# Two blocks of a transformer-like network on one core: the recurrence's gates as tanh of three fp32r products, and a fixed place on VectorE for the recurrence's second part

## The chip, the cores and the metric

One Trainium2 chip, one core. The metric is the device time of one execution in microseconds (us). The kernel takes and returns 512 tokens of width 1024 in float32.

## What is computed

The reference runs two blocks one after the other. The first (spatial gating, a gated delta rule over 64-token chunks, a mixture of 32 experts) is not touched by the change. The second puts 16 learned tokens ahead of the 512, so T = 528, and computes from the normalized tokens in parallel an attention with 8 query and 2 key heads, and a gated linear recurrence in both directions of time. Their results are merged by two gates, projected, and followed by a feed-forward layer. The recurrence is the part that matters here. For each of two directions:

```python
def rg_lru(xc, wa, ba, wx, bx, lam, reverse):
    r = sigmoid(einsum('btnc,ncd->btnd', xb, wa) + ba)   # xb: xc in 8 blocks of 128 channels
    i = sigmoid(einsum('btnc,ncd->btnd', xb, wx) + bx)
    log_a = 8.0 * r * log_sigmoid(lam)
    a = exp(log_a)
    u = sqrt(-expm1(2.0 * log_a)) * (i * xf)
    h = scan of h[t] = a[t] * h[t-1] + u[t], along time or against it
```

`xc` is a convolution over four neighbouring tokens of a projection of the input. A sigmoid is (1 + tanh(x/2)) / 2.

## The kernel before

The program is written in Python that records instructions. Tiles come from pools: `bufs` is how many buffers a name has in turn, and an instruction that writes a buffer waits until the reads of its last contents are done. In the stage of interest (`block2`, lines 1563 to 1650) the order of TensorE's instructions is the order in which they are recorded. The order on VectorE, ScalarE and SP is made by a planner, which goes by the order of recording and by when it reckons that an instruction's operands are there. Two helpers tie it: `act` (line 90) keeps ScalarE's table functions in the order of recording, and `after` puts one instruction behind others on its engine.

Matrix products that have to be exact are made with `mm3` (lines 198 to 200): both operands are split into an upper part in fp32r and a remainder (`split`: a copy on ScalarE, line 90, and a subtraction on VectorE, line 170), and three products are summed in PSUM. The views `by_turns` and `unturned` interleave the two halves of the columns, so that neighbouring columns of a product come from different halves.

The stage is a loop over n = 0 to 7. Turn n is called head n here. It joins parts of generators, each of which stops at its `yield`s:

- `gates`: three projections of 128 columns for the merge gates and the recurrence's output gate, 24 passes of 512 columns each.
- `attention` of head n: the scores for two blocks of 128 queries (`weights`; L198 to L200 into `psD`), the row maxima (L2127, L2128), the exponential (`pr`), its normalization (L2133, L2135), and in `turned` the transposes (L2141 for the 16 learned tokens, L2146 for the others) with their split into `PThi` and `PTlo`; the same again for the other two blocks; one turn later the product with the values, and one more turn later the sum with the recurrence (`ao`, L2164) and its split into `ga` and `rn`, called the mix here.
- `rnn_x` of n + 1: the projection of block n + 1 (48 passes of 264 columns), its evacuation in two halves to `xr`, and the convolution `xc` on VectorE (L2027, L2029).
- `rnn_gates` of n: eight f32 products (L2047) of 264 columns into four `psD` tiles: for each direction `rg`, then `ig`, evacuated by ScalarE as sigmoids. Then `ig` is multiplied with `xc` (L2050).
- `rnn` of n - 1, in two parts. The first makes tanh, exponential and square of the decay on ScalarE and L2093 on VectorE. The second takes two roots on ScalarE, then multiplies (L2099), scans (L2102), and adds both directions (L2104, L2105).

In a middle turn TensorE does: first projection, product with the values of head n - 1, gates of n, scores, second projection, transposes, third projection, scores, projection of block n + 1, transposes.

PSUM has two buffers of `psD` (two banks each), which the gates and the scores share, and two banks each of `psA` and `psB`. `rg`, `ig`, `wg`, `xr` and `xc` have two buffers, the root's tile `th` one. The split weights have two buffers, `whi` and `wlo`; the raw ones four, which SP loads in order.

Of the kernel before, what the change touches and what calls it, by code (L numbers as in the profile page):

```python
# [9 lines left out]
FT = mybir.dt.float32  # L10
FR = mybir.dt.float32r
I32 = mybir.dt.int32
BF = mybir.dt.bfloat16
AF = mybir.ActivationFunctionType
OP = mybir.AluOpType
# [14 lines left out]
TOKS = [slice(t * 128, (t + 1) * 128) for t in range(NT)]  # L30
# [23 lines left out]
def halves(x):  # L54

    return x.rearrange("p (s c) -> p s c", s=2)


def by_turns(x):

    return x.rearrange("p (s c) -> p c s", s=2)


def unturned(x):

    return x.rearrange("p (c s) -> p s c", s=2)
# [9 lines left out]
class Net:  # L76
# [1913 lines left out]
    def rnn_start(self, p, vec):  # L1990

        nc = self.nc
        x = vec[:, 72:88]
        cl = p.tile([128, 2, 16], FT, name="cl")
        y = p.tile([128, 16], FT, name="cl_y")
        c = cl[:, 0, :]
        nc.vector.scalar_tensor_tensor(y, x, -1.0, x, op0=OP.mult, op1=OP.min)
        self.act(y, y, AF.Exp)
        self.log1p_unit(p, c, y, 16)
        nc.vector.tensor_scalar(y, x, 0.0, None, op0=OP.min)  # L2000
        nc.vector.tensor_tensor(c, y, c, OP.subtract)
        nc.vector.tensor_scalar(c, c, 8.0, None, op0=OP.mult)
        nc.vector.tensor_scalar(cl[:, 1, :], c, -1.0, None, op0=OP.mult)
        return cl

    def rnn_x(self, p, n, vec, xT):

        nc, I = self.nc, self.I
        T = META + S
        H = T // 2  # L2010
        nhi, nlo = xT
        wg = p.tile([128, 2, 2, 128], FT, name="wg")
        nc.sync.dma_start(wg[:, 0], I["rg_wa_2"][0, :, n].rearrange("d c e -> c d e"))
        nc.sync.dma_start(wg[:, 1], I["rg_wx_2"][0, :, n].rearrange("d c e -> c d e"))
        hi, lo = self.wchunk(I["w_in_2"][0], 0, NK, 1536 + n * 128, 128)
        xr = p.tile([128, T + 3], FT, name="xr")
        nc.vector.memset(xr[:, 0:2], 0.0)
        nc.vector.memset(xr[:, T + 2:], 0.0)
        for j in range(2):
            js = slice(j * H, (j + 1) * H)  # L2020
            ps = self.psA.tile([128, 512], FT, name="psA")
            for k in range(NK):
                self.mm3(ps[:, :H], hi[:, k, :], lo[:, k, :], by_turns(nhi[:, k, js]), by_turns(nlo[:, k, js]),
                         k == 0, k == NK - 1)
            self.act(halves(xr[:, 2 + j * H:2 + (j + 1) * H]), unturned(ps[:, :H]), AF.Copy)
        c = p.tile([128, T], FT, name="xc")
        nc.vector.tensor_scalar(c, xr[:, 0:T], vec[:, n:n + 1], vec[:, 32 + n:33 + n], op0=OP.mult, op1=OP.add)  # L2027
        for j in range(1, 4):
            nc.vector.scalar_tensor_tensor(c, xr[:, j:j + T], vec[:, 8 * j + n:8 * j + n + 1], c,  # L2029
                                           op0=OP.mult, op1=OP.add)  # L2030
        return c, wg

    def rnn_gates(self, p, n, vec, x, meanwhile=lambda: None):

        nc = self.nc
        T = META + S
        H = T // 2
        c, wg = x
        rg = p.tile([128, 2, T], FT, name="rg")
        ig = p.tile([128, 2, T], FT, name="ig")  # L2040
        for d in range(2):
            if d:
                meanwhile()
            for w, dst, bias in ((0, rg, 40), (1, ig, 56)):
                ps = self.psD.tile([128, 2, 512], FT, name="psD")
                for j in range(2):
                    nc.tensor.matmul(ps[:, j, :H], wg[:, w, d, :], c[:, j * H:(j + 1) * H], start=True, stop=True)  # L2047
                self.act(dst[:, d, :].rearrange("p (a b) -> p a b", a=2), ps[:, :, :H], AF.Sigmoid,
                         bias=vec[:, bias + 8 * d + n:bias + 8 * d + n + 1])
        nc.vector.tensor_tensor(ig, ig, c[:, None, :].to_broadcast([128, 2, T]), OP.mult)  # L2050
        return rg, ig

    def gates(self, p, n, xT, rn, ga):
# [25 lines left out]
    def rnn(self, p, n, cl, st, rn):  # L2079

        nc = self.nc
        T = META + S
        rg, ig = st
        u = p.tile([128, 2, T], FT, name="th", bufs=1)
        for d in range(2):
            q = 8 * d + n
            r, t = rg[:, d, :], u[:, d, :]
            self.act(t, r, AF.Tanh, scale=cl[:, 1, q:q + 1])
            self.act(r, r, AF.Exp, scale=cl[:, 0, q:q + 1])

            a2 = p.tile([128, T], FT, name="a2", bufs=1)
            self.act(a2, r, AF.Square)
            nc.vector.scalar_tensor_tensor(t, a2, 1.0, t, op0=OP.add, op1=OP.mult)  # L2093
        yield
        for d in range(2):
            self.act(u[:, d, :], u[:, d, :], AF.Sqrt, scale=0.0625)
        for d in range(2):
            t, g, r = u[:, d, :], ig[:, d, :], rg[:, d, :]
            nc.vector.tensor_tensor(g, g, t, OP.mult)  # L2099
            if d:  # L2100
                t, g, r = t[:, ::-1], g[:, ::-1], r[:, ::-1]
            nc.vector.tensor_tensor_scan(t, r, g, 0.0, op0=OP.mult, op1=OP.add)  # L2102
        f = u[:, 0, META:]
        nc.vector.tensor_tensor(f, f, u[:, 1, META:], OP.add)  # L2104
        nc.vector.tensor_tensor(rn[n], rn[n], f, OP.mult)  # L2105
        yield

    def attention(self, tp, h, kv, rn, ga, gp, mix):
        nc = self.nc
        H = (META + S) // 2  # L2110
        khi, klo, vhi, vlo, qs = (kv[n] for n in ("khi", "klo", "vhi", "vlo", "qs"))
        g = h // 4
        qf = tp.tile([128, S], FT, name="qf")
        nc.sync.dma_start(qf, self.q_d[h])
        q = [tp.tile([128, S], FR, name="q" + n) for n in ("hi", "lo")]
        self.split(*q, qf)

        Phi = tp.tile([128, NT + 1, S], FR, name="PThi", bufs=1)
        Plo = tp.tile([128, NT + 1, S], FR, name="PTlo", bufs=1)
# [18 lines left out]
        def turned(w):  # L2138
            for t, ps, pf in w:
                pm = ps[:META, 0, H:H + 128]  # L2140
                nc.tensor.transpose(pm, pf[:, 0:META], self.ident)  # L2141
                self.split(Phi[:META, 0, TOKS[t]], Plo[:META, 0, TOKS[t]], pm)
            for t, ps, pf in w:
                pt = self.psB.tile([128, 4, 128], FT, name="psB")
                for b in range(NT):
                    nc.tensor.transpose(pt[:, b, :], pf[:, META + b * 128:META + (b + 1) * 128], self.ident)  # L2146
                self.split(Phi[:, 1:, TOKS[t]], Plo[:, 1:, TOKS[t]], pt)

        for t in (0, 2):
            w = [weights(t), weights(t + 1)]  # L2150
            yield
            turned(w)
            if t == 0:
                yield
# [179 lines left out]
```

## Time and profile before

| | |
|---|---|
| median of 3 runs | 1913.13 us (1912.49 to 1913.63) |
| the profiled execution | 1913.31 us, span 1911.5 us |
| TensorE (PE) busy | 1804.0 us, 94% of the span |
| weight loads (PEld) | 1362.2 us, 71% |
| VectorE (DVE) busy | 990.3 us, 52% |
| ScalarE (ACT) busy | 708.9 us, 37% |
| GpSimd (POOL) busy | 31.3 us, 2% |
| TensorE's clock, mean | 0.988 of full speed |
| the stage with the recurrence | about 1236 to 1545 us of the span |

Times within the span are counted from its first instruction. A matmul is recorded from its start to its modelled end, and the next one starts before that, so the distance of two starts is what a pass costs. Neighbouring VectorE and ScalarE instructions overlap in the same way. In brackets stands how long the engine was idle before an instruction, and what ended that.

### The profile page before, as it was taken

Reading aid. Unit: us, or ns where it says so; the run is one execution under the profiler, and the core shown is the slowest. Engines: PE = TensorE matmul, PEld = TensorE weight load, DVE = VectorE, ACT = ScalarE, POOL = GpSimd, SP = SyncE. Lnnn points to the kernel's source line nnn. Section 1 sums busy time; section 2 is a strip of 40 time slices with the busy share of each in tenths; the row PEclk is TensorE's granted clock in tenths of the full one; section 3 lists DMA queues with packets and bytes.
Section 4 is the critical chain, followed back from the end, with each engine's and each line's share of the span. In section 5 each row is a group of like instructions: output and inputs, shape, how many; then the busy total and the mean of one; then the engine's idle time right before and its main releaser. Section 6 shows DMA issues by size and latency. Waiting matters only on the chain. (4 is left out here: it accounts for less than half of the span.)

```text
span 1911.5 us, 23909 instructions
## 1 busy us (share of the span) xinstructions
PE 1804.0 (94%) x9309; PEld 1362.2 (71%) x9309; DVE 990.3 (52%) x1834; ACT 708.9 (37%) x1157; POOL 31.3 (2%) x39
## 2 busy tenths in 40 slices
PE   6999999989999899999898979999999999999999
PEld 5787888868898744433343337888888778888887
DVE  6843787745466623222121259658878763333332
ACT  5343444424333322111010126467677733323322
POOL 0000000100000000000000000000000000000000
PEclk9999999989999899999999999999999999999999
DMA  8645776875378689999999873432221233333331
GB/s 255 99 117 101 121 93 82 156 175 77 90 271 332 243 347 423 424 425 425 424 425 425 368 279 122 137 89 83 78 66 56 88 101 110 100 104 105 99 122 66
DMA packets 251988, 368.20 MB, mean 193 GB/s; under 512 B 31328, under 2 KB 193665, under 8 KB 227938
## 3 DMA queue, kind: packets, MB, share of 16 engines
q1 hardware_dynamic: 241218, 342.79, 56.3%
q10 hardware_dynamic: 7632, 16.78, 2.3%
q0 software_dynamic: 3024, 7.09, 1.0%
q8 instruction: 74, 1.21, 0.3%
q14 instruction: 40, 0.33, 0.0%
HBM read 348.51 MB, written 22.04 MB: 194 GB/s over the span
## 5 line engine op out<-in xcount | busy, mean ns | idle before, releaser
L90 ACT ACTIVATE whi<-raw 128x1024 fp32r<-128x1024 f32 (+1 forms) x203 | 233.4, 1155 | 417.4 <-PE psA L199 266.8
L170 DVE TENSOR_TENSOR wlo<-raw,whi 128x1024 fp32r<-128x1024 f32 (+1 forms) x195 | 249.5, 1280 | 243.2 <-ACT whi L90 229.5
L1289 PE MATMUL psB<-mwt,XT 128*64 128x512 f32 x1008 | 233.7, 598 | 7.9 <-DMA mwt<-in_w 5.5
L1289 PEld LDWEIGHTS psB<-mwt,XT 128*64 128x64 f32 x1008 | 76.6, 138 | 153.1 <-issue 135.3
L200 PE MATMUL psA<-hT_hi,wlo 128*128 128x512 f32 (+1 forms) x456 | 176.2, 386 | 10.0 <-DVE wlo L170 10.0
L199 PE MATMUL psA<-hT_lo,whi 128*128 128x512 f32 (+1 forms) x456 | 177.6, 389 | 0.0
L198 PE MATMUL psA<-hT_hi,whi 128*128 128x512 f32 (+1 forms) x456 | 176.1, 386 | 0.9 <-ACT whi L90 0.9
L1354 DVE TENSOR_TENSOR res<-res,psA 128x512 f32<-128x512 f32 x128 | 79.3, 679 | 125.0 <-PE psA L1349 125.0
L1322 PE MATMUL psB<-mwt,hbT 128*64 128x512 f32 x480 | 118.0, 596 | 21.1 <-DMA mwt<-in_w 19.8
L198 PE MATMUL psA<-hn_hi,whi 128*128 128x512 f32 (+1 forms) x368 | 136.5, 371 | 0.2 <-ACT hn_hi L90 0.2
L199 PE MATMUL psA<-hn_lo,whi 128*128 128x512 f32 (+1 forms) x368 | 136.4, 371 | 0.3 <-DVE hn_lo L2198 0.3
L200 PE MATMUL psA<-hn_hi,wlo 128*128 128x512 f32 (+1 forms) x368 | 136.3, 370 | 0.0
L198 PE MATMUL psA<-xn_hi,whi 128*128 128x512 f32 (+1 forms) x320 | 109.4, 342 | 0.4 <-ACT qx L90 0.4
L1298 DVE TENSOR_TENSOR sl<-sl,psB 128x512 f32<-128x512 f32 x16 | 11.0, 688 | 188.0 <-PE psB L1289 188.0
L200 PE MATMUL psA<-xn_hi,wlo 128*128 128x512 f32 (+1 forms) x320 | 108.2, 338 | 0.0
L199 PE MATMUL psA<-xn_lo,whi 128*128 128x512 f32 (+1 forms) x320 | 108.1, 338 | 0.0
L1322 PEld LDWEIGHTS psB<-mwt,hbT 128*64 128x64 f32 x480 | 36.1, 136 | 97.0 <-issue 58.0
L200 PEld LDWEIGHTS psA<-hT_hi,wlo 128*128 128x128 f32 (+1 forms) x456 | 86.3, 189 | 22.7 <-DVE wlo L170 11.0
L198 PEld LDWEIGHTS psA<-hT_hi,whi 128*128 128x128 f32 (+1 forms) x456 | 86.1, 189 | 13.6 <-ACT whi L90 1.3
L199 PEld LDWEIGHTS psA<-hT_lo,whi 128*128 128x128 f32 (+1 forms) x456 | 86.1, 189 | 11.9
L90 ACT ACTIVATE XT<-psA 128x512 f32<-128x512 f32 x32 | 17.5, 594 | 205.0 <-PE psA L1266 199.5
L199 PEld LDWEIGHTS psA<-hn_lo,whi 128*128 128x128 f32 x368 | 69.6, 189 | 9.5 <-DVE hn_lo L2198 0.5
(571 smaller groups left out, 3489.7 us busy)
## 6 DMA issues: line engine op xcount, KB each, us to landing
mwt<-in_w SPq DMA_DIRECT2D x188, 1024.0 KB, 20.1
raw<-in_w_in SPq DMA_DIRECT2D x108, 512.0 KB, 7.1
raw<-in_w_ffn_in SPq DMA_DIRECT2D x44, 512.0 KB, 3.9
raw<-in_w_ffn_out SPq DMA_DIRECT2D x22, 512.0 KB, 3.6
raw<-in_w_pa SPq DMA_DIRECT2D x8, 512.0 KB, 6.1
raw<-in_w_pb SPq DMA_DIRECT2D x8, 512.0 KB, 4.9
raw<-in_w_o SPq DMA_DIRECT2D x8, 512.0 KB, 11.8
raw<-in_w_out SPq DMA_DIRECT2D x8, 512.0 KB, 3.6
```

What stands on the lines that cost most here:

```text
L90: ins = self.nc.scalar.activation(out, in_, func, **kw)
L170: return self.nc.vector.tensor_tensor(lo, x, hi.bitcast(FT), OP.subtract)
L198: nc.tensor.matmul(out, whi, xhi, start=first, stop=False)
L199: nc.tensor.matmul(out, whi, xlo, start=False, stop=False)
L200: nc.tensor.matmul(out, wlo, xhi, start=False, stop=last)
L1289: nc.tensor.matmul(ps[CAP * i:CAP * (i + 1), :], XT[:, r0 + k, CAP * i:CAP * (i + 1)], w_, start=(r0 + k == 0), stop=(r0 + k == NK - 1))
L1298: nc.vector.tensor_tensor(so, so, h[1], OP.mult)
L1322: nc.tensor.matmul(pys[half][CAP * i:CAP * (i + 1), :], hT[:, r0 + k, CAP * i:CAP * (i + 1)], ws[i][:, k, half * 512:(half + 1) * 512], st ...
L1354: nc.vector.tensor_tensor(x, x, unturned(ps), OP.add)
```

## The change

`rnn_gates` makes the gates with `mm3` from split weights and a split `xc`, and evacuates them with tanh(x/2) through the view by turns. `rnn_x` therefore splits the gates' weights (into `wghi`, one buffer, and a second tile named `wg`) and `xc` (into a second tile named `xr` and `xclo`, one buffer); `xc` has one buffer instead of two. The constants take over the halves and the ones: the decay's factor is halved and also given as bias, the gate biases are halved once, the root's scale is a quarter of what it was, and `ig` is multiplied as (ig + 1) * c. Behind the two roots a tanh of one column is added. The first product of each direction in the second part is put behind the last lower part of the attention weights (`self.low`).

```diff
--- before.py
+++ after.py
@@ -1999,7 +1999,9 @@
         self.log1p_unit(p, c, y, 16)
         nc.vector.tensor_scalar(y, x, 0.0, None, op0=OP.min)
         nc.vector.tensor_tensor(c, y, c, OP.subtract)
-        nc.vector.tensor_scalar(c, c, 8.0, None, op0=OP.mult)
+        nc.vector.tensor_scalar(c, c, 4.0, None, op0=OP.mult)
+
+        nc.vector.tensor_scalar(vec[:, 40:72], vec[:, 40:72], 0.5, None, op0=OP.mult)
         nc.vector.tensor_scalar(cl[:, 1, :], c, -1.0, None, op0=OP.mult)
         return cl
 
@@ -2012,6 +2014,8 @@
         wg = p.tile([128, 2, 2, 128], FT, name="wg")
         nc.sync.dma_start(wg[:, 0], I["rg_wa_2"][0, :, n].rearrange("d c e -> c d e"))
         nc.sync.dma_start(wg[:, 1], I["rg_wx_2"][0, :, n].rearrange("d c e -> c d e"))
+        ws = p.tile([128, 2, 2, 128], FR, name="wghi", bufs=1), p.tile([128, 2, 2, 128], FR, name="wg")
+        self.split(*ws, wg)
         hi, lo = self.wchunk(I["w_in_2"][0], 0, NK, 1536 + n * 128, 128)
         xr = p.tile([128, T + 3], FT, name="xr")
         nc.vector.memset(xr[:, 0:2], 0.0)
@@ -2023,19 +2027,21 @@
                 self.mm3(ps[:, :H], hi[:, k, :], lo[:, k, :], by_turns(nhi[:, k, js]), by_turns(nlo[:, k, js]),
                          k == 0, k == NK - 1)
             self.act(halves(xr[:, 2 + j * H:2 + (j + 1) * H]), unturned(ps[:, :H]), AF.Copy)
-        c = p.tile([128, T], FT, name="xc")
+        c = p.tile([128, T], FT, name="xc", bufs=1)
         nc.vector.tensor_scalar(c, xr[:, 0:T], vec[:, n:n + 1], vec[:, 32 + n:33 + n], op0=OP.mult, op1=OP.add)
         for j in range(1, 4):
             nc.vector.scalar_tensor_tensor(c, xr[:, j:j + T], vec[:, 8 * j + n:8 * j + n + 1], c,
                                            op0=OP.mult, op1=OP.add)
-        return c, wg
+        cs = p.tile([128, T + 3], FR, name="xr")[:, 0:T], p.tile([128, T], FR, name="xclo", bufs=1)
+        self.split(*cs, c)
+        return c, cs, ws
 
     def rnn_gates(self, p, n, vec, x, meanwhile=lambda: None):
 
         nc = self.nc
         T = META + S
         H = T // 2
-        c, wg = x
+        c, (chi, clo), (whi, wlo) = x
         rg = p.tile([128, 2, T], FT, name="rg")
         ig = p.tile([128, 2, T], FT, name="ig")
         for d in range(2):
@@ -2044,10 +2050,13 @@
             for w, dst, bias in ((0, rg, 40), (1, ig, 56)):
                 ps = self.psD.tile([128, 2, 512], FT, name="psD")
                 for j in range(2):
-                    nc.tensor.matmul(ps[:, j, :H], wg[:, w, d, :], c[:, j * H:(j + 1) * H], start=True, stop=True)
-                self.act(dst[:, d, :].rearrange("p (a b) -> p a b", a=2), ps[:, :, :H], AF.Sigmoid,
+                    js = slice(j * H, (j + 1) * H)
+                    self.mm3(ps[:, j, :H], whi[:, w, d, :], wlo[:, w, d, :], by_turns(chi[:, js]), by_turns(clo[:, js]),
+                             True, True)
+                self.act(dst[:, d, :].rearrange("p (a s c) -> p a s c", a=2, s=2),
+                         ps[:, :, :H].rearrange("p a (c s) -> p a s c", s=2), AF.Tanh, scale=0.5,
                          bias=vec[:, bias + 8 * d + n:bias + 8 * d + n + 1])
-        nc.vector.tensor_tensor(ig, ig, c[:, None, :].to_broadcast([128, 2, T]), OP.mult)
+        nc.vector.scalar_tensor_tensor(ig, ig, 1.0, c[:, None, :].to_broadcast([128, 2, T]), op0=OP.add, op1=OP.mult)
         return rg, ig
 
     def gates(self, p, n, xT, rn, ga):
@@ -2085,18 +2094,21 @@
         for d in range(2):
             q = 8 * d + n
             r, t = rg[:, d, :], u[:, d, :]
-            self.act(t, r, AF.Tanh, scale=cl[:, 1, q:q + 1])
-            self.act(r, r, AF.Exp, scale=cl[:, 0, q:q + 1])
+            self.act(t, r, AF.Tanh, scale=cl[:, 1, q:q + 1], bias=cl[:, 1, q:q + 1])
+            self.act(r, r, AF.Exp, scale=cl[:, 0, q:q + 1], bias=cl[:, 0, q:q + 1])
 
             a2 = p.tile([128, T], FT, name="a2", bufs=1)
             self.act(a2, r, AF.Square)
             nc.vector.scalar_tensor_tensor(t, a2, 1.0, t, op0=OP.add, op1=OP.mult)
         yield
         for d in range(2):
-            self.act(u[:, d, :], u[:, d, :], AF.Sqrt, scale=0.0625)
+            self.act(u[:, d, :], u[:, d, :], AF.Sqrt, scale=0.25 ** 3)
+
+        self.act(self.small.tile([128, 1], FT, name="warm"), cl[:, 0, 0:1], AF.Tanh)
         for d in range(2):
             t, g, r = u[:, d, :], ig[:, d, :], rg[:, d, :]
-            nc.vector.tensor_tensor(g, g, t, OP.mult)
+
+            self.after(nc.vector.tensor_tensor(g, g, t, OP.mult), self.low)
             if d:
                 t, g, r = t[:, ::-1], g[:, ::-1], r[:, ::-1]
             nc.vector.tensor_tensor_scan(t, r, g, 0.0, op0=OP.mult, op1=OP.add)
@@ -2144,7 +2156,7 @@
                 pt = self.psB.tile([128, 4, 128], FT, name="psB")
                 for b in range(NT):
                     nc.tensor.transpose(pt[:, b, :], pf[:, META + b * 128:META + (b + 1) * 128], self.ident)
-                self.split(Phi[:, 1:, TOKS[t]], Plo[:, 1:, TOKS[t]], pt)
+                self.low = self.split(Phi[:, 1:, TOKS[t]], Plo[:, 1:, TOKS[t]], pt)
 
         for t in (0, 2):
             w = [weights(t), weights(t + 1)]
```

## Rows read from the trace of the kernel before

PE is TensorE, DVE VectorE, ACT ScalarE. Head 4 is a middle turn.

**Rows 1.** busy time: stretch, length, each engine (instructions), TensorE clock, DMA

```profile
1370.26:1404.95 34.69, 33.60 (x197) 29.14 (x195) 27.77 (x52) 25.53 (x45) 0.00 (x0) 1.00 0.27 77
```

**Rows 2.** waits of TensorE, 1236 to 1545 us: total, times, longest

```profile
PE psD L198 <- ACT rg L90: 5.4, 6, 1.0
PE psD L198 <- DVE PTlo L170: 3.0, 2, 1.8
```

**Rows 3.** timeline of TensorE, head 4: start, length, instruction, idle before

```profile
1380.16 3.89 PE L2047 MATMUL psD<-xc,wg 128*128 128x264 f32 x16
1385.02 0.38 PE L198 MATMUL psD<-kThi,qhi 128*128 128x264 f32 x1 [0.96 <-ACT rg L90]
...
1391.65 0.67 PE L2141 MATMUL psD<-ident,pr 128*16 128x128 f32 x2
```

**Rows 4.** timeline of TensorE, head 1

```profile
1276.93 3.89 PE L2047 MATMUL psD<-xc,wg 128*128 128x264 f32 x16
1280.72 0.38 PE L198 MATMUL psD<-kThi,qhi 128*128 128x264 f32 x1
```

**Rows 5.** timeline of TensorE, head 4's last projection passes

```profile
1368.01 0.28 PE L199 MATMUL psA<-xn_lo,whi 128*128 128x264 f32 x1
1368.12 0.28 PE L200 MATMUL psA<-xn_hi,wlo 128*128 128x264 f32 x1
```

**Rows 6.** timeline of ScalarE, head 4

```profile
1369.36 1.28 ACT L90 ACT_TABLE_LOAD   x1
...
1371.74 0.37 ACT L90 ACTIVATE xr<-psA 128x264 f32<-128x264 f32 x1
...
1379.13 1.28 ACT L90 ACT_TABLE_LOAD   x1 [1.56 <-DVE th L2102]
1381.25 0.70 ACT L90 ACTIVATE rg<-psD,vec 128x528 f32<-128x528 f32 x1 [0.83 <-PE psD L2047]
...
1383.74 0.63 ACT L90 ACTIVATE ga<-ao 128x512 fp32r<-128x512 f32 x1 [0.90 <-DVE xr L2018]
1384.28 0.68 ACT L90 ACTIVATE rg<-psD,vec 128x528 f32<-128x528 f32 x1
...
1388.22 1.28 ACT L90 ACT_TABLE_LOAD   x1 [2.18 <-DVE m L2128]
1389.52 0.79 ACT L90 ACTIVATE pr<-psD,m,qs 128x528 f32<-128x528 f32 x1
```

**Rows 7.** timeline of VectorE, head 4

```profile
1371.33 1.33 DVE L2099 TENSOR_TENSOR ig<-ig,th 128x528 f32<-128x528 f32 x2 [0.28 <-ACT th L90]
1372.58 0.55 DVE L2027 TENSOR_SCALAR xc<-xr,vec 128x528 f32<-128x528 f32 x1
...
1376.67 2.38 DVE L2102 TENSOR_TENSOR_SCAN th<-rg,ig 128x528 f32<-128x528 f32 x2
...
1383.04 0.67 DVE L2164 TENSOR_TENSOR ao<-ao,rn 128x512 f32<-128x512 f32 x1
...
1384.41 0.69 DVE L170 TENSOR_TENSOR rn<-ao,ga 128x512 fp32r<-128x512 f32 x1 [0.68 <-ACT ga L90]
1385.59 1.26 DVE L2050 TENSOR_TENSOR ig<-ig,xc 128x1056 f32<-128x1056 f32 x1 [0.49 <-ACT ig L90]
...
1388.00 0.28 DVE L2128 SCALAR_TENSOR_TENSOR m<-m,qs 128x1 f32<-128x1 f32 x2
...
1391.41 0.49 DVE L2135 TENSOR_SCALAR pr<-pr,s 128x528 f32<-128x528 f32 x1
```

**Rows 8.** VectorE's groups, 1236 to 1545 us: count, busy us, mean ns

```profile
L170 DVE TENSOR_TENSOR qlo<-qf,qhi 128x512 fp32r<-128x512 f32 x8 | 5.4, 677 | 1.8 <-ACT qhi L90 1.8
```

**Rows 9.** timelines of ScalarE and TensorE, the stage's tail

```profile
1520.52 1.28 ACT L90 ACT_TABLE_LOAD   x1 [2.97 <-DVE rn L2105]
...
1522.99 0.72 ACT L90 ACTIVATE rg<-rg,cl 128x528 f32<-128x528 f32 x1
...
1537.01 0.48 PE L198 MATMUL psD<-whi,ga 128*128 128x512 f32 x1 [2.01 <-ACT ga L90]
```

## The prediction

> **What bounds the kernel now.** Only the stage of the second block is touched in which the eight heads of attention and the eight blocks of the recurrence run together; I read it in this order. First the busy time of one steady head, from one pair of transposes to the same pair a head later [rows 1]: 34.69 us, of which TensorE is busy 33.60, VectorE 27.77 and ScalarE 25.53, at full granted clock. So TensorE sets the pace and VectorE is the next. Then the list of TensorE's waits [rows 2]: one line stands out, the first score matmul that waits for ScalarE's evacuation of a gate, 6 times, 5.4 us. Then that place in the timelines of TensorE, ScalarE and VectorE for head 4 [rows 3, 6, 7]. The reader should see three things.
>
> One: the gates' sixteen passes start at 1380.16 and the scores at 1385.02, 4.86 us later, the last 0.96 idle [rows 3]. In head 1, which has no earlier head's mix to split, the same passes start at 1276.93 and the scores at 1280.72, 3.79 us [rows 4]. The difference of 1.07 is ScalarE's order: the mix's upper part (`ga<-ao`) stands ahead of the second direction's `rg`, and it starts only at 1383.74, when VectorE's sum (1383.04 and 0.67 long) is there [rows 6, 7].
>
> Two: ScalarE loads three activation tables per head, 1.28 us each, at 1369.36 (root), 1379.13 (sigmoid) and 1388.22 (exponential) [rows 6]. Only the third delays something: the row maxima are scaled at 1388.28 [rows 7], and the exponential starts at 1389.52. The second weights are normalized at 1391.41 + 0.49 = 1391.90 [rows 7]; TensorE is at their transposes at 1391.65 [rows 3] and waits there about 0.3.
>
> Three: from 1371.33 to 1388.28 VectorE has almost no gap: products, convolution, lower parts, two scans, two weight splits, four elementwise steps, the gates' product, the maxima [rows 7]. The sigmoid's table load waited for the scans (they end at 1379.05), since the gate buffer is the one that they read [rows 6, 7].
>
> **The change, part by part.** The sum is made against the profiled execution, 1913.31 us with a span of 1911.5; the median of the runs is 1913.13, so they can be used alike.
>
> *Gate matmuls.* Eight f32 products, recorded as sixteen passes that occupy 3.89 us [rows 3], become 24 fp32r passes. Such passes of 264 columns start 0.11 us apart [rows 5]: 24 x 0.113 = 2.70. But there are two score buffers, so the third gate waits for the first one's evacuation: six passes 0.68; evacuation starts 0.2 later (1381.25 less 1380.16 leaves 1.09, of which four passes are about 0.9) and lasts 0.70 as now [rows 6], or 0.79, what the exponential takes that reads PSUM in the same pattern [rows 6]; 0.05 to release; third gate 0.68; 0.2; 0.70 to 0.79; 0.05. Together 3.25 to 3.45; I take 3.4. Against 3.79 that is 0.4 gained. Against 4.86 it is 1.46, if ScalarE no longer holds `rg` behind the mix. I take that it doesn't: the gate is ready about 2.6 us after the block's start, the mix's sum about 4.9 after it (1385.1, worked out with the last rival but one), so a planner that takes what is ready first has them the other way round. The reverse is a rival.
>
> Each pass has its weight load, 195 in a head and 29.14 us busy [rows 1]; passes with loads start 0.11 apart all the same [rows 5], so the eight more loads cost nothing of their own.
>
> *Sigmoid to tanh.* Tanh and exponential follow each other without a load at the tail, 1520.52 to 1522.99 [rows 9]; the load ahead of that tanh serves both. So the loads at 1379.13 and 1388.22 become one, issued by the new tanh on one element behind the roots. That one costs 1.28 where ScalarE has nothing urgent (behind the attention weights' upper parts), and the exponential starts 1.28 earlier relative to the maxima. The load occupies 1.28 and the next instruction starts at once (1388.22 + 1.28, then 1389.52) [rows 6]. The Trainium skill, ScalarE: Activation LUTs, What ACT_TABLE_LOAD costs, adds a drain of 1380 ns to each switch; by it the exponential would start 2.66 us earlier, TensorE's 1.8 per head would come through, and the time be the first rival's 1900.5. The trace disagrees: 0.02 from the load's end to the exponential, so 1.28 stands.
>
> *Splits.* Per head ScalarE gets two more copies (0.63 each, as the mix's copy of that size [rows 6]) and VectorE two more subtractions (0.68 each, start to start about 0.62), by the queries' split of the same size [rows 8]. ScalarE's 1.26 is paid by the 1.28 saved. The weights' split can go into VectorE's pauses around the exponentials, if not it costs 0.62; it is taken as 0. The convolution's split lies between the convolution and the gates, so its 0.62 lies in the dense stretch. The weights' load now waits for the previous split instead of the gates two blocks back; SP issues it in order, with other weight loads behind it, but that split is done most of a head before the next one is wanted, so 0. The biases' halving, 16-column work before the stage, 0. The product with (gate + 1) is taken at the 1.26 of the product that it replaces [rows 7]; nothing shows the other form at this width.
>
> *The tie.* The two products (1.33 [rows 7]) no longer run ahead of the convolution, but behind the last lower part. They ran in a pause in which VectorE waited for the second half of `xr` (1371.74 + 0.37 = 1372.11 [rows 6]). Convolution and lower parts therefore come about 0.4 earlier, and the scans later: their start moves from 1376.67 by -0.45 + 1.25 + 0.62 to 1378.1, their end to 1380.5. The gates' first evacuation, ready at about 1380.6, still just misses it. This tie alone gains nothing: TensorE waited for lower parts only twice, 3.0 us in all [rows 2], at the end of the stage, not in steady heads.
>
> *Sum.* VectorE's stretch from 1372.58 to 1388.28 was 15.70, with pauses of 0.68 and 0.49 [rows 7]. With the products (1.25) and the split (0.62) in and the pauses out it is 16.40, begun at 1372.11: the maxima are ready at 1388.5, 0.2 later than now. The exponential starts then, 1.0 earlier than 1389.52, and the second weights are normalized at 1390.9. TensorE, 1.46 earlier, would be there at 1390.2, so it waits for VectorE: a steady head gains 1.0 to 1.1, not 1.46 + 0.3. Five steady heads (2 to 6): 5.3. Head 1: 0.4 + 0.3 = 0.7. Head 7, whose gates lie on both sides of another product: 1.0. Head 0, where the longer way from convolution to gates eats most: 0.3. The tail: the last tanh's load, which waited for the last scan's product (1520.52), goes, and TensorE there waited 2.01 for the mix [rows 9]: 1.28, less some 0.3 for weight splits behind the new load, so 1.0. Together 8.3, so I forecast 1905.0.
>
> **The rivals.**
> *VectorE isn't the limit.* The planner puts the maxima ahead of the mix's steps, or the split of c in a pause. Then a steady head gains 1.46 + 0.3, say 1.8, five of them 9.0; with head 1's 0.7, head 7's 1.8 and 1.3 at the ends that is 12.8: 1900.5. For it: the mix is needed much later. Against: its steps come earlier in the program than the maxima. The same time would follow if a table load held ScalarE for longer than its record, which no row shows; 0.02 of the chance below is for that.
> *The load is only moved.* If the new tanh goes straight behind the roots, the second `xr` is out 1.5 later (the load and one short instruction), and VectorE's stretch with it: the maxima at 1390.0 and the exponential 0.5 later than now. Five heads lose 0.5, the ends gain 2: 1913.5. Against it: `xr` and the upper parts are earlier in the program and ready by then.
> *The mix stays ahead of the gate (slower).* With the stretch longer, the sum ends at 1383.71 + 1.4 = 1385.1 instead, the copy (0.54), `rg` and the release follow, and the scores start at 1386.4, 1.4 later than now. Less 0.3 for the transposes, each of five steady heads loses 1.1, head 7 about 0.8, less 2 at the ends: 1917.6. It decides as soon as the sum ends later than 1384.4 and the order is as now.
> *c is split late.* If its lower part is placed behind the scans (1381), the gates' second pass waits about 0.7; but that is what TensorE waits at the transposes anyway, so it changes the place of the wait and not the forecast.
>
> **How the numbers follow.** Forecast 0.42, VectorE not the limit 0.28, moved load 0.16, mix ahead 0.14. The range runs from 1897 (the second case, with 3.5 us for the forms that no row shows and the weights' split in a pause) to 1914.5 (past the moved load) and leaves out the slower case. A measurement tells about 0.2% (3.8 us) from no change. Faster by more: the first two cases, 0.70; within: the moved load and the milder part of the mix ahead, 0.18; slower: the rest, 0.12.
>
> **What would show it.** Two table loads per head, none ahead of the exponentials; gates' fp32r passes 0.113 apart; scores 3.3 to 3.5 after the gates' start, `rg` ahead of the mix's copy on ScalarE; scans ending near 1380.5 on this scale; a wait of TensorE at the transposes for the normalized weights of about 0.7. Steady heads of about 33.6 would bear out the sum; heads of 34.7 or more, with the mix's copy still ahead of `rg`, or `xr` behind a table load, would prove it wrong.

## The result, and the profile after

| | before | after |
|---|---|---|
| median (runs) | 1913.13 us (9) | 1921.78 us (9) |
| profiled execution, span | 1913.31, 1911.5 us | 1919.51, 1917.6 us |
| TensorE's clock, mean | 0.988 | 0.982 |

The ratio is 1.0055, 95% interval 1.0041 to 1.0069: the change makes the kernel slower by 8.65 us, by more than 0.2%. The forecast was 1905.0.

The loss lies in the stage with the recurrence. From head 0's gates to the first transposes of the last projection's result it took 308.55 us before (1241.21 to 1549.76) and 319.29 after (1236.53 to 1555.82): 10.74 more. The stages ahead of it were 4.68 shorter in the profile after. Of the change there lie only 16-column work and the first head's splits, and the kernel before and e7_tiles_before, whose code is the same up to there, reach head 0's gates at 1241.21 and 1245.63; so that is what one execution differs from another. The starts of the gates show where in the stage it goes (distance from gates n to gates n + 1, and from head 7's gates to those transposes; the lower rows belong to experiments):

| kernel | 0 | 1 | 2 | 3 | 4 | 5 | 6 | 7 to the end |
|---|---|---|---|---|---|---|---|---|
| before | 35.72 | 33.94 | 34.60 | 34.69 | 34.70 | 34.68 | 31.06 | 69.16 |
| after | 35.73 | 33.47 | 35.46 | 36.39 | 35.45 | 36.55 | 34.01 | 72.23 |
| e1_tiles | 35.73 | 33.48 | 34.86 | 34.31 | 34.33 | 34.32 | 31.40 | 69.01 |
| e15_scans_first | 36.88 | 33.48 | 34.90 | 34.47 | 34.44 | 34.47 | 31.60 | 69.20 |
| e9_tiles_notie | 35.73 | 34.70 | 35.39 | 37.08 | 34.69 | 37.07 | 32.29 | 72.17 |
| e13_last_head | 35.73 | 33.05 | 34.14 | 33.62 | 33.62 | 33.61 | 30.69 | 68.65 |

Only head 1 got shorter, by 0.5: it has no earlier scans to wait for, and its scores come 3.36 after its gates instead of 3.79. TensorE's waits of after (1236 to 1545 us; total, times, longest), which answer to [rows 2]:

```profile
PE psD L198 <- ACT rg L90: 12.3, 6, 2.1
PE psD L198 <- DVE PTlo L170: 3.4, 2, 1.8
PE psD L198 <- ACT whi L90: 2.6, 1, 2.6
```

The one wait that the change was to shorten is 12.3 us instead of 5.4, and it sits in another place: ahead of the third gate, no longer ahead of the scores. Of the 12.3, 1.8 lie in head 0, which waited 1.7 there before too; heads 2 to 6 wait 2.1 each. TensorE in head 4 of after, beside [rows 3]:

```profile
1377.58 0.28 PE L198 MATMUL psD<-xr,wghi 128*128 128x264 f32 x1
...
1381.19 0.38 PE L198 MATMUL psD<-xr,wghi 128*128 128x264 f32 x1 [2.10 <-ACT rg L90]
...
1382.93 0.38 PE L198 MATMUL psD<-kThi,qhi 128*128 128x264 f32 x1
...
1390.00 0.38 PE L2153 MATMUL psD<-ident,pr 128*16 128x128 f32 x2
```

Twelve passes, two gates, are through within 1.5 us. Then TensorE stands for 2.10, because the first gate is still in its PSUM buffer. The scores come 5.35 after the gates' start; before it was 4.86, and 3.4 was forecast. Why the evacuation is late is on ScalarE, beside [rows 6]:

```profile
1366.58 1.28 ACT L90 ACT_TABLE_LOAD   x1
1367.88 1.18 ACT L90 ACTIVATE th<-th 128x528 f32<-128x528 f32 x2
1369.06 1.28 ACT L90 ACT_TABLE_LOAD   x1
1370.36 0.20 ACT L90 ACTIVATE warm<-cl 128x1 f32<-128x1 f32 x1
1370.46 0.37 ACT L90 ACTIVATE xr<-psA 128x264 f32<-128x264 f32 x1
...
1380.44 0.70 ACT L90 ACTIVATE rg<-psD,vec 128x528 f32<-128x528 f32 x1 [4.37 <-DVE th L2114]
1381.04 0.69 ACT L90 ACTIVATE ig<-psD,vec 128x528 f32<-128x528 f32 x1
1382.17 0.70 ACT L90 ACTIVATE rg<-psD,vec 128x528 f32<-128x528 f32 x1 [0.44 <-PE psD L200]
1382.77 0.62 ACT L90 ACTIVATE wghi<-wg 128x512 fp32r<-128x512 f32 x1
1383.30 0.69 ACT L90 ACTIVATE ig<-psD,vec 128x528 f32<-128x528 f32 x1
...
1384.35 0.64 ACT L90 ACTIVATE ga<-ao 128x512 fp32r<-128x512 f32 x1
...
1386.55 0.79 ACT L90 ACTIVATE pr<-psD,m,qs 128x528 f32<-128x528 f32 x1 [1.56 <-DVE m L2140]
```

Three things. ScalarE is idle for 4.37 us ahead of the first `rg`, and what ends it is `th`, a scan: the new `rg` goes into the buffer that the scans of the head before read as their factor. The second table load stands straight behind the roots, so the second half of `xr` waits for it. And the two forecast gains are there: the mix's copy is behind the second `rg`, and no load stands ahead of the exponential. VectorE, beside [rows 7]:

```profile
1370.87 0.55 DVE L2031 TENSOR_SCALAR xc<-xr,vec 128x528 f32<-128x528 f32 x1 [2.25 <-ACT xr L90]
...
1374.97 0.69 DVE L2111 TENSOR_TENSOR ig<-ig,th 128x528 f32<-128x528 f32 x1
1375.59 0.69 DVE L170 TENSOR_TENSOR xclo<-xc,xr 128x528 fp32r<-128x528 f32 x1
1376.21 1.24 DVE L2114 TENSOR_TENSOR_SCAN th<-rg,ig 128x528 f32<-128x528 f32 x1
1377.38 0.67 DVE L2111 TENSOR_TENSOR ig<-ig,th 128x528 f32<-128x528 f32 x1
1377.97 1.20 DVE L170 TENSOR_TENSOR wlo<-raw,whi 128x1024 fp32r<-128x1024 f32 x1
1379.11 1.24 DVE L2114 TENSOR_TENSOR_SCAN th<-rg,ig 128x528 f32<-128x528 f32 x1
```

The second scan ends at 1380.35, and `rg` starts 0.09 later. Between the scans stands a weight split of 1.2 us for the projection that begins only at 1384.82. Before, the second scan ended 1.11 ahead of the gates' start [rows 3, 7]; now it ends 2.77 behind it.

And TensorE's clock. Windows of after (stretch, length, TensorE, its weight loads, VectorE, ScalarE, GpSimd, clock, DMA), the first two a head each, beside [rows 1]:

```profile
1381.19:1416.65 35.46, 33.07 (x203) 29.33 (x203) 28.46 (x54) 25.74 (x47) 0.00 (x0) 1.00 0.23 68
1344.81:1381.19 36.38, 34.28 (x203) 30.86 (x203) 28.53 (x54) 25.84 (x47) 0.00 (x0) 0.95 0.25 72
1345.00:1350.00 5.00, 5.00 (x27) 4.86 (x27) 3.78 (x8) 3.27 (x6) 0.00 (x0) 0.66 0.56 165
1300.00:1545.00 245.00, 225.34 (x1268) 197.42 (x1268) 194.05 (x341) 172.31 (x293) 0.00 (x0) 0.95 0.25 75
```

A head takes 35.46 at full clock and some 36.4 when the clock falls behind the wait. Right behind the wait of 2.11 that ends at 1344.81, the passes of 264 columns come 0.22 apart instead of 0.11:

```profile
1344.81 0.38 PE L198 MATMUL psD<-xr,wghi 128*128 128x264 f32 x1 [2.11 <-ACT rg L90]
...
1345.31 0.43 PE L198 MATMUL psD<-xr,wghi 128*128 128x264 f32 x1
1345.53 0.43 PE L199 MATMUL psD<-xclo,wghi 128*128 128x264 f32 x1
```

That is the lower of two levels, 1.2 instead of 2.4 GHz. The Trainium skill, TensorE: Matmul & The Clock Gate, What's actually happening, says that there are just these two and that the engine's own activity decides; the spacing here, 0.22 and 0.11, agrees with the two levels. Before, the clock over 1300 to 1500 was 1.00, and over the whole stretch:

```profile
1300.00:1545.00 245.00, 231.80 (x1283) 198.86 (x1282) 196.18 (x338) 174.82 (x288) 0.00 (x0) 0.99 0.27 81
```

### The profile page after: what moved, and what is told of

Read it like the earlier page. It is cut to its first block, busy times and chain, and to the rows that moved or that the text cites. A ratio compares the mean times of both kernels' runs of the same rounds, so it can differ in the third digit from the quotient of the medians.

```text
span 1917.6 us, 24080 instructions
## 1 busy us (share of the span) xinstructions
PE 1807.7 (94%) x9373; PEld 1371.3 (72%) x9373; DVE 997.7 (52%) x1851; ACT 712.4 (37%) x1174; POOL 31.2 (2%) x39
## 5 line engine op out<-in xcount | busy, mean ns | idle before, releaser
L198 PEld LDWEIGHTS psA<-hn_hi,whi 128*128 128x128 f32 x368 | 69.6, 189 | 9.5 <-ACT hn_hi L90 0.5
```

What stands on the lines that cost most here:

```text
L198: nc.tensor.matmul(out, whi, xhi, start=first, stop=False)
```

## Experiments

Theory A: the wait is for `rg`'s buffer, that is for the second scan, and everything put ahead of that scan on VectorE is paid by TensorE, partly twice, by the clock. Rivals: B, VectorE's whole stretch is the limit, so the wait only moves; C, the three-pass gates are dear in themselves or bring the clock down. Each kernel ran beside the kernel before on the same chip, whose median stands second.

| run | median, before | ratio (95%) | clock 1300 to 1545 |
|---|---|---|---|
| e1_tiles | 1911.11, 1912.18 | 0.9996 (0.998 to 1.0013) | 0.99 |
| e2_notie | 1923.51, 1912.18 | 1.0058 (1.0038 to 1.0078) | 0.96 |
| e3_nowarm | 1936.24, 1912.18 | 1.0119 (1.0087 to 1.0152) | 0.94 |
| e4_warmlate | 1925.78, 1912.18 | 1.0072 (1.0049 to 1.0096) | 0.95 |
| e5b_sig_notie | 1924.91, 1914.94 | 1.0048 (1.003 to 1.0067) | 0.97 |
| e6b_tanh_notie | 1922.6, 1914.94 | 1.0037 (1.0021 to 1.0053) | 0.99 |
| e7_tiles_before | 1914.66, 1914.94 | 0.9991 (0.9979 to 1.0004) | 0.99 |
| e12_ties_mix | 1910.98, 1914.94 | 0.9985 (0.9971 to 0.9999) | 0.99 |
| e9_tiles_notie | 1924.71, 1912.53 | 1.0065 (1.0041 to 1.009) | 0.96 |
| e13_last_head | 1908.17, 1912.53 | 0.9972 (0.9958 to 0.9985) | 0.99 |
| e14_dense_between | 1929.44, 1912.53 | 1.0081 (1.0057 to 1.0105) | 1.00 |
| e15_scans_first | 1911.85, 1915.46 | 0.9991 (0.9975 to 1.0006) | 0.99 |

**e1_tiles**: after, with `rg` and `ig` in one tile per direction, so that the first evacuation waits for the first scan only. The product of `ig` with `xc` then comes in two instructions.

```diff
-        rg = p.tile([128, 2, T], FT, name="rg")
+        rg = [p.tile([128, T], FT, name=f"rg{d}") for d in range(2)]
...
-        nc.vector.scalar_tensor_tensor(ig, ig, 1.0, c[:, None, :].to_broadcast([128, 2, T]), op0=OP.add, op1=OP.mult)
+        for d in range(2):
+            nc.vector.scalar_tensor_tensor(ig[d], ig[d], 1.0, c, op0=OP.add, op1=OP.mult)
```

> The changed kernel, with the gates of the two directions in tiles of their own (rg0, rg1, ig0, ig1), so that the evacuation of the first direction's gates waits only for the first scan, not for both. Theory A (the gates' first evacuation waits for the second scan, since both directions share a buffer, TensorE stands 2.1 us and its clock falls behind that): the wait at the third gate falls from 2.1 us to under 0.5 in heads 2 to 6, no granted clock under 1.00 from 1300 to 1500, about 15 us less than the changed kernel: 1902 to 1910. Rival B (VectorE has more work than a head has room for): the wait only moves to the scores or the transposes, heads stay over 34.7 us, 1913 or more. Rival C (the clock falls because of the three-pass gates, not because of the wait): low clock in the same places, 1910 to 1916.

TensorE's waits in it, and the first evacuation of head 4 on ScalarE:

```profile
PE psD L2154 <- DVE pr L2148: 4.2, 5, 1.0
PE psD L198 <- ACT rg L90: 2.1, 2, 1.8
```

```profile
1379.90 0.70 ACT L90 ACTIVATE rg<-psD,vec 128x528 f32<-128x528 f32 x1 [2.90 <-PE psD L200]
```

The wait on `rg` goes from 12.3 to 2.1, and 1.75 of that is head 0's; in heads 2 to 6 only one of 0.38 is left. What ends ScalarE's idle time ahead of the first `rg` is now TensorE and no longer a scan. The clock from 1300 to 1500 is back at 1.00, and the scores start 3.37 after the gates (1379.02 to 1382.39), the forecast's 3.4. What stays is the wait for the normalized weights at the transposes, 0.8 to 1.0 in five heads, which the forecast named. So A holds, and behind it B; the total lies 1 us above A's range. Against the kernel before it is no gain.

**e15_scans_first**: after, its tiles as they are (both directions in one), with the second projection's weight split tied behind the second scan.

```diff
-        self.act(halves(g), self.dense_fm(w_in, 4608 + n * 128, real), AF.Tanh, scale=0.5)
+        self.act(halves(g), self.dense_fm(w_in, 4608 + n * 128, real, (self.scan,) if n > 1 else ()), AF.Tanh, scale=0.5)
...
-            nc.vector.tensor_tensor_scan(t, r, g, 0.0, op0=OP.mult, op1=OP.add)
+            self.scan = nc.vector.tensor_tensor_scan(t, r, g, 0.0, op0=OP.mult, op1=OP.add)
```

> The kernel after, tiles and all, with one thing moved: the second projection's lower weight part (1.2 us on VectorE) is tied behind the second scan instead of standing between the two scans. Theory A (the first gate's evacuation waits for the second scan, and what stands ahead of that scan on VectorE is the price): the second scan ends 1.1 us sooner, the wait on rg falls from 2.1 to about 1.0 us in six heads (12.3 to 6 or 7 us in all), the granted clock is back at 1.00 between 1300 and 1500, middle heads take 34.3 to 34.8 us, and the time is that of the kernel before or of e1_tiles: 1910 to 1914 us, ratio 0.998 to 1.002. Rival (the clock falls for another reason than these waits, the denser passes for instance): heads over 35 us, clock below 0.97, 1917 us or more. Second rival (the lower weight part is then late for its projection): the wait on rg falls and one of the same size comes up on wlo, 1918 to 1922.

A wait of TensorE, the second scan and the split of head 4 on VectorE, and a window (head 4):

```profile
PE psD L198 <- ACT rg L90: 5.5, 6, 1.8
```

```profile
1376.63 1.26 DVE L2114 TENSOR_TENSOR_SCAN th<-rg,ig 128x528 f32<-128x528 f32 x1
1377.81 1.20 DVE L170 TENSOR_TENSOR wlo<-raw,whi 128x1024 fp32r<-128x1024 f32 x1
```

```profile
1376.59:1411.03 34.44, 33.11 (x204) 29.28 (x203) 28.44 (x56) 25.87 (x46) 0.00 (x0) 1.00 0.24 70
```

As A has it: one instruction of 1.2 us in another place, and the whole loss is gone. In heads 3 to 6 the wait is 0.64 to 0.66 instead of 2.1. The passes are the same 24, so C falls: they do not bring the clock down.

**e7_tiles_before**: the kernel before with e1's tiles, as a control.

> Control: the kernel before with rg and ig in a tile for each direction and the product with c split in two. The scans end at 1379.05 in the kernel before and the first evacuation waits for its table load until 1380.41, so theory A expects nothing: 1910.5 to 1914 us, ratio 0.999 to 1.001, scores still waiting about 1 us on rg behind the mix's copy. If separate tiles were good by themselves (not through the scan that the first evacuation waits for): below 1909 us.

No difference in the time, as expected: where the scans are early, the buffer costs nothing. The wait behind the mix's copy is 1.25 a head instead of 0.95, but the middle heads take 34.70 as before.

**e2_notie** (after without the tie) and **e9_tiles_notie** (e1 without it):

```diff
-            self.after(nc.vector.tensor_tensor(g, g, t, OP.mult), self.low)
+            nc.vector.tensor_tensor(g, g, t, OP.mult)
```

> The changed kernel without the tie: products and scans may run ahead of the convolution and of the lower parts. In VectorE's order they then stand ahead of the whole convolution. Theory A: the wait at the third gate is gone, but the lower parts come some 3 us later and TensorE waits for them, or for c's split, ahead of the product with the values: 2 to 3 us per head there, low clock again, 1918 to 1930. If the tie is what costs (rival D): 1900 to 1910.

> The split tiles of e1_tiles without the tie of the products to the weights' lower parts. Without the tie the kernel after had waits of 1.0 us on PTlo in five heads in place of part of those on rg (e2_notie). Theory A: with split tiles rg is no longer waited for, the tie alone decides whether the first half of VectorE's work delays the upper product's PTlo: a wait on PTlo of about 1 us in five heads, 1911.1 + 5 = 1916 us (1913 to 1918), against 1911 with the tie. The forecast's statement that the tie gains nothing: 1910 to 1912.5 us and no wait on PTlo beyond the 3.4 us in two of e1_tiles.

Waits in e9_tiles_notie:

```profile
PE psB L198 <- DVE PTlo L170: 5.2, 5, 1.0
PE psD L198 <- ACT rg L90: 4.2, 4, 1.8
```

With the shared tile the tie makes no difference that the intervals show (1.0058 against 1.0055): without it 5.2 us on `PTlo` in five heads and 4.4 on `rg` stand in place of 12.3 on `rg`. So the tie is not what costs. With split tiles it is worth 0.7% of the time, some 13 us (1.0065 against 0.9996): both products and the first half of VectorE's work then delay `PTlo`, and the clock falls in heads 3 and 5 (37.08 and 37.07, of which 0.8 is a wait on `rg`, against 34.69 in head 4). The expectation, 1916, had the wait on `PTlo`, but neither the one on `rg` (0.8 in three heads) nor the clock.

**e3_nowarm**: after without the one-column tanh.

```diff
-        self.act(self.small.tile([128, 1], FT, name="warm"), cl[:, 0, 0:1], AF.Tanh)
```

> The changed kernel without the one-column tanh: the table is loaded when the first gate is evacuated. Theory A: the scans end about 1.4 us earlier, but the load of 1.28 follows them, so the first evacuation is where it was; and the mix's copy stands ahead of the second rg again, which costs up to 1 us more: 1920 to 1928. If only the load's early place was at fault: 1906 to 1912.

The expectation failed at its first step: the scans do not come earlier. A weight copy on ScalarE and a weight split on VectorE take the load's old place, `xc` starts 6.70 ahead of the gates (6.71 in after), and the second scan ends 2.77 behind their start, as in after. The load then stands behind that scan, directly ahead of `rg` (its idle time before it ends with `th`): wait on `rg` 3.4 in five heads, 18.8 in all with head 0's 1.8, and heads of 37.9 to 38.0. So the wait is longer by the load's 1.28, and the clock falls in each of heads 2 to 6 (0.95 or 0.96 over each of heads 2 to 5). The mix's copy, ahead of the second `rg` again, costs nothing here: that `rg` waits for TensorE behind it.

**e4_warmlate**: the one-column tanh tied behind the last upper part, where the prediction had it.

> The changed kernel, with the one-column tanh behind the last upper part of the attention weights on ScalarE, so that the second half of xr is evacuated before its table load. Theory A, with the load's place as the cause of 1.4 of the 2.1 us: the convolution and the scans come 1.4 us earlier, the wait at the third gate falls to about 0.7, the clock stays up in most heads: 1906 to 1912. If the place of the load counts for nothing (B): within 3 us of the changed kernel.

A's number for it was wrong; the time is near after's (1.0072 against 1.0055, intervals that overlap), as if the load's place counted for nothing. The wait on `rg` is 12.3 in 6, as in after: in the load's old place ScalarE's planner put a weight copy (1.04) ahead of the second `xr`, and VectorE's a weight split (1.22) ahead of `xc`; `xc` starts 6.70 ahead of the gates, in after 6.71. Taking away one piece ahead of the scan helps only if nothing else is put there.

**e5b_sig_notie**: the three passes and the splits alone, with sigmoid, three loads, no tie. **e6b_tanh_notie**: the tanh alone, with f32 products.

> The three passes with their splits alone: sigmoid gates, three table loads per head, no tie, no one-column tanh. Theory A (what counts is when ScalarE can evacuate a gate, not how long the products take): the mix's copy stands between the two rg evacuations again and its ao comes 0.6 us later than before (one more split, 0.68 us, between VectorE's scans), so the scores wait about 2.2 to 2.8 us on rg in six heads and the granted clock falls behind those waits: 1914 to 1922 us. Theory C of the study (three-pass products are dear in themselves or lower the clock by themselves): slower as well, but with waits on rg of 1 us or less and the clock below 0.97 all through 1300 to 1500. The forecast's own sum for the products alone (gates 3.89 to 1.8 us, no new wait): 1905 to 1909 us.

> Tanh gates with the one-column tanh alone: f32 products, no splits of c and of the gates' weights, no tie. Both scans stand ahead of xc on VectorE, so rg's buffer is free long before the gates. Theory A: no wait over 1 us on rg, two table loads per head, the exponentials without a load; 1906 to 1912 us. If the tanh by itself costs (the second half of xr behind a second table load, rival 'the load is only moved'): xc late, a wait on xc or xr at the gates in every head, 1913 to 1919 us.

In e5b_sig_notie TensorE waits at the scores, and ScalarE shows for what (timelines of head 4, TensorE and then ScalarE):

```profile
1390.88 0.38 PE L198 MATMUL psD<-kThi,qhi 128*128 128x264 f32 x1 [2.22 <-ACT rg L90]
```

```profile
1386.29 0.70 ACT L90 ACTIVATE rg<-psD,vec 128x528 f32<-128x528 f32 x1
...
1389.61 0.63 ACT L90 ACTIVATE ga<-ao 128x512 fp32r<-128x512 f32 x1 [2.02 <-DVE xr L2021]
1390.15 0.68 ACT L90 ACTIVATE rg<-psD,vec 128x528 f32<-128x528 f32 x1
```

Here the mix does stay ahead of the gate, the prediction's slower rival. The scores wait 2.1 to 2.2 in five heads, about what A expected; the time, 1924.9, lies above its range. In e6b_tanh_notie A's number was wrong and the other one nearer (1922.6, its range ends at 1919), though the wait is not on `xr` itself: 1.0 on `PTlo` in five heads, since VectorE does both products and both scans (1371.12 to 1374.67 in one head) ahead of `xc` and the lower parts, and 0.9 on `rg` in five, behind the mix. So each half of the change loses by itself, and each through the order of other work.

**e12_ties_mix** and **e13_last_head** try to keep the gain. To e1 come: the third projection's lower weight part behind the scores' maxima, the gates' weight copy behind the last gate, the mix recorded behind the scores; then, in e13, the first of these not in head 7, and no one-column tanh behind head 7's roots.

```diff
+                        next(g)
+                        next(a)
                         if old:
                             next(old)
-                        next(g)
-                        next(a)
...
-        self.split(*ws, wg)
+        self.after(self.act(ws[0], wg, AF.Copy), *([self.lastg] if n > 1 else []))
+        nc.vector.tensor_tensor(ws[1], wg, ws[0].bitcast(FT), OP.subtract)
...
-        ps = self.dense_fm(w_in, 2560 + n * 128, real)
+        ps = self.dense_fm(w_in, 2560 + n * 128, real, (self.red,) if n + 1 < NK else ())
...
-        self.act(self.small.tile([128, 1], FT, name="warm"), cl[:, 0, 0:1], AF.Tanh)
+        if n + 1 < NK:
+            self.act(self.small.tile([128, 1], FT, name="warm"), cl[:, 0, 0:1], AF.Tanh)
```

> The split tiles of the run e1_tiles, and VectorE's stretch behind the gates relieved: the third projection's lower weight part behind the scores' maxima instead of ahead of them (1.2 us off the way to pr), the gates' weight copy behind the last gate, the mix issued behind the scores. Theory A with VectorE's stretch as the limit: the waits at the transposes on pr (4.2 us in 5) fall to 1 us or less, that on ig (1.2 in 6) to 0.3; 1911.1 - 4 = 1907 us, range 1904.5 to 1909, ratio 0.996 to 0.9985. If the waits only move on (to PTlo or whi): 1910 to 1912.

> e12_ties_mix with the tie of the weights' lower part taken off the last head (there it put 2.0 us on wlo and 0.9 on ig into TensorE's waits) and without the one-column tanh behind the last head's roots (one table load fewer ahead of the output projection, whose wait on whi was 2.6 us). Theory A (each of these waits stands on TensorE's way): 2.5 + 1 to 1.5 us less than e12_ties_mix, ratio 0.9965 (0.995 to 0.998). If the last head's waits only move: as e12_ties_mix, 0.9985.

Waits of e13_last_head, and a window (head 4):

```profile
PE psD L198 <- ACT whi L90: 2.6, 1, 2.6
PE psD L198 <- ACT rg L90: 2.1, 2, 1.8
PE psD L2156 <- DVE pr L2150: 1.4, 5, 0.5
```

```profile
1378.18:1411.80 33.62, 33.02 (x205) 29.20 (x203) 28.32 (x55) 25.97 (x46) 0.00 (x0) 1.00 0.24 71
```

The wait for `pr` falls from 4.2 to 1.4, a head takes 33.62, and e13 beats both kernels: 4.4 us under the kernel before by the medians, 0.28% by the ratio. e12 itself comes out at the edge of its range (0.9985), with `pr` at 1.4 and `ig` at 1.1 where 1 or less and 0.3 were expected. In e12 head 7 had lost 2.9 us at the tied split; with the tie off there, that came back. The tanh left out bought nothing: the wait on `whi` at the tail stays at 2.6. What of e12 each of its three edits brings was not taken apart.

**e14_dense_between**: e13, with the second projection between the gates' two directions.

```diff
-                        st = self.rnn_gates(rp, n, vec, x)
-                        next(g)
+                        st = self.rnn_gates(rp, n, vec, x, lambda: (next(g), next(g)))
...
-                        next(g)
```

> e13_last_head with the second projection issued between the gates' two directions, so that TensorE has work while ScalarE evacuates the first two gates; scores, third projection and transposes follow. In e12_ties_mix the gates' block took 3.36 us for 1.8 us of passes in each of seven heads. Theory A (the block is bound by the evacuations): up to 1.5 us less in six heads, 7 us, ratio 0.993 (0.991 to 0.997), if no new wait comes up. Rival: the third projection comes 2.6 us sooner after the gates and then waits for its lower weight part (tied behind the maxima), or PTlo and pr come late: ratio 0.997 to 1.003, with waits on wlo or PTlo of over 1 us in five heads.

The rival won, by more than its range: 15.4 us on `PTlo` and 12.0 on `wlo`, and heads of 37.15. The third projection now comes before its lower weight part is ready, and the second scores follow the transposes within 3.1 us (1406.69 and 1409.74), before the PSUM buffer that they share is read out.

## Why the prediction was wrong

The failed step is in "The tie": that the scans would end at 1380.5 and the gates' first evacuation "still just misses it", so that `rg`'s buffer costs nothing. On the scale of before (gates at 1380.16, that is 2.58 more than in after) the scans end at 1382.93, 2.4 later than forecast, and the evacuation meets them. The 2.4 is made of:

- *The load's place.* It was to lie "behind the attention weights' upper parts" where ScalarE has nothing urgent. It went straight behind the roots, as in the rival "The load is only moved": `xc` starts at 1370.87 + 2.58 = 1373.45, not 1372.11: 1.3 late.
- *What stands between the scans.* They were taken as one piece of 2.38, as in [rows 7]. The tie put the second product (0.6) between them instead of ahead of both, which alone changes nothing, and the planner filled in a weight split: 1.14. It was not in the stretch's order because the order was taken from before.

1.3 + 1.14 = 2.44. The evacuation was due 0.88 behind the gates' start (1379.02 and 1379.90 in e1_tiles), as the prediction's own 0.68 and 0.2 have it: 1381.04 on this scale, not the 1380.6 that it names. So 1.9 of the 2.4 came through, and with the release that is the wait of 2.1. The rival that had the load right priced it at 0.5 per head, by VectorE's stretch to the maxima; it missed the buffer as well. The second failed step is the sum itself: it has no term for the clock, which it takes as full. The waits of 2.1 make heads of 35.46, +0.77 over before; the heads with a fall are at 36.4 to 36.6, twice that and more. At the stage's end, too (72.23 against 69.16), the clock is 0.89 in 1486 to 1513, behind waits of 1.17 and 0.78 for `xr` and `xclo` at head 7's gates, and TensorE waits 1.54 for `PTlo`.

The other terms did not come either where the buffer is free. In e1_tiles the stage takes 307.44 (1240.64 to 1548.08), 1.1 less than before, not 8.3. Heads 3 to 5 gain some 0.37 each instead of 1.0 to 1.1; the load's place and the order of the splits on VectorE are as in after. Head 6 loses 0.34, as TensorE waits 0.53 for `xr` at head 7's gates. And the tail's 1.0 is missing: TensorE's wait of 2.01 for the mix is gone, but one of 2.58 for a weight copy (`whi`) has come up, in after and in e1_tiles alike; that copy stands on ScalarE behind the roots' table load (1526.74 after 1524.37 in e1_tiles).

What was right:

- The gates' block of 3.4 us if its evacuations are free: 3.37 in e1_tiles. As forecast, it is the two buffers in turn that make it longer than the 2.70 of passes: `rg` at 1379.90, the third gate at 1380.65, the second `rg` at 1381.63, the scores at 1382.39.
- `rg` ahead of the mix's copy; two loads per head, none ahead of the exponential, which starts 0.10 after the scaled maximum (1386.55 after 1386.30 + 0.15). The load is 1.28 and the next instruction starts 0.02 later (1369.06 and 1370.36). The Trainium skill, ScalarE: Activation LUTs, What ACT_TABLE_LOAD costs, adds a drain of 1380 ns to each switch; no load here shows it, and the trace decides.
- VectorE as the next limit, with about 0.7 of wait at the transposes: 0.8 to 1.0 in e1_tiles. In after itself it isn't seen, since the wait at the gates comes first: the weights are normalized at 1389.52, and TensorE is at the transposes at 1390.00.
- "Steady heads of about 33.6" only in number: 33.62 in e13_last_head, where the tiles are split, two splits moved and the mix recorded later, with the load still behind the roots. That is another order than the forecast's, so the agreement does not bear out its sum; e1_tiles has 34.3.
- "This tie alone gains nothing" is right for the changed kernel (e2_notie) and wrong as soon as the buffer is free (e9_tiles_notie).

The rival "VectorE isn't the limit", with heads some 1.8 shorter, did not occur in any run. "c is split late" did not in after either: the split stands between the first product and the first scan.

## What to carry to other kernels

When a producer is made faster, look for what its output buffer still waits for: a buffer that two directions share is free only when the last of its readers is done, and that reader sits in another engine's queue. When operations are added to a nearly full queue that a planner orders, write down the new order piece by piece up to the one instruction that releases something, and price a slip at that point; tie the pieces with slack behind it. And leave room in the sum for TensorE's clock where the change can lengthen TensorE's waits: here it fell behind three of the five waits of 2.1 in after, and around two of the five of 1.04 in e9_tiles_notie.

## What the runs showed that was not expected

The clock's price. In after, a wait of 2.1 us costs a head up to 1.1 us more (36.55 against 35.45) through the lower clock behind it. But its length doesn't settle it: in after the wait of 2.10 ahead of 1381.19 was followed by a clock of 1.00 (1380 to 1385), the one ahead of 1416.65 by 0.69 (1415 to 1420). In e9_tiles_notie a wait of 1.04 on `PTlo`, ahead of 1375.34, stands in a window of 0.71 (1375 to 1380), the same wait ahead of 1411.72 in one of 1.00 (1410 to 1415), and in e14_dense_between waits of 1.72 and 1.80 in each of heads 1 to 6 left it at 1.00 throughout (1300 to 1500). What else decides it, no run here separates.

A scan of 528 columns takes 1.24 us on VectorE where a product of the same size takes 0.69, so in a stretch of elementwise work the scans are the pieces to count double.
